# The last layer's modulations in block 2: one of three units in the first attention and two in the second, instead of two and one

## The chip, the cores and the metric

The kernel is one program on one core of a Trainium2 chip. The metric is the time of one execution on the device in microseconds; less is better. Times are medians of several executions, and one further execution was taken with the hardware profiler.

## The reference, cut to what matters

The model is a chain of two blocks of two layers each, on 256 tokens of width 1024, in float32. In block 2 each layer is an attention mixer followed by a hierarchical mixture of experts (MoE), and both are modulated by six vectors that come from the conditioning vector `c_2` alone:

```
cs = jax.nn.silu(c)
for l in range(DEPTH):                       # DEPTH = 2
    mod = (cs @ ada_w[l] + ada_b[l])[:, None, :]
    sh1, sc1, g1, sh2, sc2, g2 = jnp.split(mod, 6, axis=-1)
    h = rms_norm_2(x, norm1_g[l]) * (1.0 + sc1) + sh1
    y = even_mixer_2(...) if l % 2 == 0 else odd_mixer_2(...)
    x = x + g1 * y
    h = rms_norm_2(x, norm2_g[l]) * (1.0 + sc2) + sh2
    x = x + g2 * hier_moe(h, ...)
```

`ada_w[l]` is 1024 x 6144. Nothing in `mod` depends on the tokens, so the product for layer 1 can be computed at any time before layer 1 needs it: `sh1` and `sc1` when layer 1 begins, `g1` when its mixer is added to `x`, and `sh2`, `sc2` and `g2` when its MoE begins.

## The kernel before, in words

Block 2 runs `layerB(0)` (mixer `even2`: four pairs of MoBA heads, four differential heads) and then `layerB(1)` (mixer `odd2`: NSA attention in eight head pairs). In each, the mixer is followed by `out2`, the output projection with the router, and then by the MoE. A head pair consists of score matmuls (`causal_scores`, lines L1561 to L1584; the matmul itself is on L200), a softmax on ScalarE (exponentials, L1581) and VectorE, TensorE transposes of the probabilities (L1592) with VectorE copies (L1593), and value matmuls (L200 with a 64-row `po` tile, or L1643 in the differential heads). In `odd2` the value matmuls read the probabilities from `PT` in the even pairs and from `x` in the odd ones.

The product `cs @ ada_w[l]` is made by generators in three **units**. A unit is one call of `ada_wide`: eight loads of 1 MB (`wraw<-in_bdaU`, from SyncE's queue), and for each load four matmuls of 32 x 512 (`ada<-wraw,csil`, L247), which stand on four column groups of the array. That makes 32 matmuls a unit; the trace holds two records for each, so 64. After every second matmul the generator yields, which is one **step**: 16 steps a unit. Unit 0 (`mods2`) gives `sh1` and `sc1` as columns. Units 1 and 2 (`wide_rows`) give `g1`, `sh2` and then `sc2`, `g2` as rows: VectorE adds the bias (`adb`, L284, for unit 2 also L290) and GpSimd's queue writes the rows to DRAM (`rows_bda`, L293), from where `gates`, `mo_c` and `mo_row` are loaded.

`causal_scores` advances the generator that stands in `self.side` by some steps, `tick(steps, i)`, and each matmul of those steps is put behind the score matmul `i` on TensorE. `even2` calls it 16 times with 2 steps, then with 2 steps in the first two differential heads (4 calls) and with 0 in the last two; `flush()` behind the mixer runs the unit that is under way to its end, and `do()` runs all that is left. `odd2` calls it 16 times with 3 steps. `self.ada2(1)` is started when layer 0 begins and is kept in `self.side` through both layers.

The final order of each engine's instructions isn't the order of the code: the framework's scheduler sorts them along a timeline of its own, and what the code fixes are data dependences, the anchors of `tick` and the buffers of the pools. Two pools matter here. `wr` has ten buffers of 1 MB for all weights, in order of use. `pa` has two PSUM banks (`ada` tiles), of which a unit holds one until its result is read, and the head pairs use the same two for their `po`.

Of the kernel before, what the change touches and what calls it, by code (L numbers as in the profile page):

```python
# [17 lines left out]
P = 128  # L18
# [1483 lines left out]
class B2(L1):  # L1502
# [15 lines left out]
    def ada2(self, l):  # L1518

        yield from self.mods2(l)  # L1520
        r = self.A[f"bdab_r{l}"]
        yield from self.wide_rows(f"bda{l}", 1, self.cs2, (2, 3), r[0], None, None, (0,))
        yield from self.wide_rows(f"bda{l}", 2, self.cs2, (4, 5), r[1], r[2], 1.0, (0,))
# [144 lines left out]
    def odd2(self, hT, ph):  # L1668
# [13 lines left out]
        ksw = [self.T(self.ar, [P, 2, S], f"ksw{n}") for n in range(2)]  # L1682
# [34 lines left out]
        qT = self.T(self.ar, [P, 8, S], "nq")  # L1717
# [34 lines left out]
        for q in range(2):  # L1752
            pr = slice(64 * q, 64 * q + 64)
# [16 lines left out]
        for t in range(2):  # L1770
# [3 lines left out]
            sc = self.S2([P, 16, 32])  # L1774
# [23 lines left out]
        for j in range(8):  # L1798
            po = self.T(self.pa, [P, S], "ada")
            if j % 2:  # L1800
                x = self.T(self.ar, [P, 2048], "x8").rearrange("p (h n k s) -> p h n k s", h=2, n=2, k=2)
                PTs = [[x[:, h2, n] for n in range(2)] for h2 in range(2)]
            else:
                PTs = [[self.T(self.ar, [P, 2, S], "PT", bufs=4) for _ in range(2)] for _ in range(2)]
            hs = [(h2, heads[j][h2], slice(64 * h2, 64 * h2 + 64)) for h2 in range(2)]
            for t in range(2):
                sc = self.causal_scores(t, [[(qT[pr, j, t * P:(t + 1) * P], ksw[n][pr, j // 4, :]) for n in range(2)] for _, _, pr in hs], 3)
                for (e, rs), (h2, h, _) in zip(sc, hs):
                    nc.vector.tensor_tensor(rs, rs, gt[:, t, h * 3 + 1:h * 3 + 3], ALU.mult)
                    for n in range(2):  # L1810
                        nc.vector.tensor_scalar(e[:, n, :], e[:, n, :], rs[:, n:n + 1], None, ALU.mult)
                        self.transp(e[:, n, :], t, PTs[h2][n])
            mm = self.chain()
            for step in range(5):
                for h2, h, pr in hs:
                    g, r = h // 4, h % 4
                    if step == 2:
                        q = slice(32 * r, 32 * r + 16)
                        mm(po[pr, :], vc[q, g, :], PcT[q, g, :], start=False, stop=False, tile_position=(32 * r, 64 * h2), skip_group_check=True)
                    else:  # L1820
                        n, kt = step % 3, step // 3
                        mm(po[pr, kt * P:], vsw[n][:, kt, g * 64:g * 64 + 64], PTs[h2][n][:, kt, kt * P:], start=step == 0, stop=step == 4,
                           tile_position=(0, 64 * h2), skip_group_check=True)
            nc.scalar.activation(mh[:, j, :], po, AF.Copy)
            nc.vector.tensor_tensor(ml[:, j, :], po, mh[:, j, :].bitcast(F32), ALU.subtract)
# [273 lines left out]
    def layerB(self, l):  # L2099
        nc, A = self.nc, self.A  # L2100
        xs = self.xs[:2]
        with self.phase() as ph:
            self.ar = ph.pool(f"arB{l}")
            self.ws = ph.pool(f"wsB{l}", 2)
            Ac, Bc = self.bmods[l]
            if l == 0:
                self.at, self.side = "unit", self.ada2(1)
            hT = self.norm_mod_T(xs, Ac, Bc, [0, 0], rs=self.rn)
            mix = (self.even2 if l == 0 else self.odd2)(hT, ph)
            if l:  # L2110
                self.do(self.side)
            else:
                self.flush()
            G = self.T(self.ar, [P, D], "gates", bufs=1)
            self.row(G, f"bda{l}", 2, 0)
            logits = self.out2(mix, A["b_out"] if l == 0 else A["n_out"], xs, G, *self.router(l))
        with self.phase(ns2=5) as ph:
            self.ar = ph.pool(f"arM{l}")
            hs = [self.T(self.ar, [P, 2, D], n, F32R) for n in ("mo_hh", "mo_hl")]
            xd = [self.T(self.ar, [P, KT, 256], "mo_xd", bufs=2) for _ in range(1)]  # L2120
            hb = [self.T(self.ar, [P, D], f"mo_h{t}") for t in range(2)]
            rows = []
            for b in (4, 3, 5):
                rows.append(self.T(self.ar, [P, D], f"mo_row{b}"))
                self.row(rows[-1], f"bda{l}", b, 0)
            if l:
                fg = self.T(self.ar, [P, D], "mo_fin")
                nc.gpsimd.dma_start(fg, A["fin_g"].partition_broadcast(P))
                self.fin = fg, hb
            self.rn = self.moe(xs, l, logits, rows, hb, *hs)  # L2130
            if l:
                for t in range(2):
                    if t:
                        nc.vector.tensor_scalar(hb[t], hb[t], self.rn[t], None, ALU.mult)
                    else:
                        nc.scalar.activation(hb[t], hb[t], AF.Copy, scale=self.rn[t])  # L2136
                    nc.sync.dma_start(self.out[t * P:(t + 1) * P, :], hb[t])
# [54 lines left out]
```

## Time and profile before

| | |
|---|---|
| median of 3 executions | 2209.05 us (2208.09 to 2222.83) |
| the profiled execution | 2220.42 us |
| its span, first to last instruction | 2218.6 us |
| TensorE matmuls busy | 2024.2 us, 91% of the span |
| VectorE, ScalarE, GpSimd busy | 55%, 38%, 6% |
| mean granted TensorE clock | 0.92 of full speed |

The profiled execution is one among those that spread over 0.7%; durations are read from it and differences are applied to the median. A busy TensorE isn't a TensorE at its peak: the ends of its matmuls are modelled and overlap.

### The profile page before, as it was taken

The page shows a single profiled execution, that of the slowest core. Times are in us where ns is not written, and L with a number is a line of the kernel's source. Part 1 is how long each engine was busy: PE and PEld are TensorE (multiplying, and loading weights), DVE is VectorE, ACT ScalarE, POOL GpSimd, SP SyncE. Part 2 cuts the span into 40 slices and gives each one's busy share as a digit, 9 for nine tenths or more (in the row PEclk, how much of TensorE's full clock was granted, in tenths as well). Part 3 has the DMA queues.
Part 4 walks back from the last instruction along what each step waited for, and adds up shares of the span by engine and source line. Part 5 has one row for each costly group of instructions (what it writes and reads, how often), then busy time and mean ns, then how long its engine had stood idle before and what let it go on. Part 6 is the DMA issues. An engine that isn't in the chain of part 4 may idle for free. (4 is left out here: it accounts for less than half of the span.)

```text
span 2218.6 us, 32046 instructions
## 1 busy us (share of the span) xinstructions
PE 2024.2 (91%) x12738; PEld 1436.3 (65%) x12738; DVE 1219.3 (55%) x2508; ACT 832.4 (38%) x1609; POOL 123.4 (6%) x229
## 2 busy tenths in 40 slices
PE   7999899999989997999987699989989989989896
PEld 4864688888866576765655589978464458546542
DVE  2247565655675645874846555666652244754423
ACT  4334443322353355565434454444341133322211
POOL 1100000001121000000110000000000010000000
PEclk8999999999999998569998899999979999968898
DMA  7546223345532345547984545364748957602494
GB/s 297 140 165 251 95 95 143 143 171 190 209 116 95 109 138 181 152 144 237 297 261 137 205 152 190 143 255 146 267 172 322 386 205 261 222 1 95 196 378 167
DMA packets 124947, 417.44 MB, mean 188 GB/s; under 512 B 19536, under 2 KB 58096, under 8 KB 90096
## 3 DMA queue, kind: packets, MB, share of 16 engines
q1 hardware_dynamic: 54064, 314.86, 38.1%
q10 hardware_dynamic: 55552, 50.95, 7.5%
q0 software_dynamic: 15168, 49.44, 6.6%
q8 instruction: 104, 1.70, 0.3%
q14 instruction: 59, 0.48, 0.1%
HBM read 386.31 MB, written 28.89 MB: 187 GB/s over the span
## 5 line engine op out<-in xcount | busy, mean ns | idle before, releaser
L192 DVE TENSOR_TENSOR wlo<-wraw,whi 128x1024 fp32r<-128x1024 f32 x252 | 308.3, 1226 | 326.6 <-ACT whi L189 326.1
L189 ACT ACTIVATE whi<-wraw 128x1024 fp32r<-128x1024 f32 x252 | 265.7, 1059 | 494.9 <-PE mm L217 236.5
L215 PE MATMUL mm<-hT_h,whi 128*128 128x256 f32 (+1 forms) x832 | 267.7, 333 | 2.5 <-ACT whi L189 2.4
L216 PE MATMUL mm<-hT_l,whi 128*128 128x256 f32 (+1 forms) x832 | 267.8, 329 | 0.0
L217 PE MATMUL mm<-hT_h,wlo 128*128 128x256 f32 (+1 forms) x832 | 242.2, 327 | 1.6 <-DVE wlo L192 1.4
L215 PEld LDWEIGHTS mm<-hT_h,whi 128*128 128x128 f32 x832 | 157.6, 191 | 20.2 <-ACT whi L189 4.1
L216 PEld LDWEIGHTS mm<-hT_l,whi 128*128 128x128 f32 x832 | 158.7, 191 | 14.8
L217 PEld LDWEIGHTS mm<-hT_h,wlo 128*128 128x128 f32 x832 | 149.5, 191 | 18.0 <-DVE wlo L192 3.2
L216 PE MATMUL mm<-wlo,b 128*128 128x512 f32 x384 | 151.7, 395 | 0.6 <-DVE wlo L192 0.6
L217 PE MATMUL mm<-whi,b 128*128 128x512 f32 x384 | 151.3, 394 | 0.0
L2040 PE MATMUL ada<-wraw,mo_xd 128*64 128x512 f32 x512 | 135.5, 599 | 0.0
L215 PE MATMUL mm<-whi,b 128*128 128x512 f32 x384 | 135.4, 394 | 0.0
L247 PE MATMUL ada<-wraw,csil 128*32 128x512 f32 x512 | 103.7, 635 | 12.3 <-DMA wraw<-in_bdaU 10.7
L402 PE MATMUL tr<-s,x 128*128 128x128 f32 x288 | 56.4, 344 | 51.2 <-DVE s L393 25.1
L216 PE MATMUL mm<-wlo,hT_h 128*128 128x512 f32 (+1 forms) x256 | 100.0, 393 | 1.5 <-DVE wlo L192 1.4
L215 PE MATMUL mm<-whi,hT_h 128*128 128x512 f32 (+1 forms) x256 | 95.9, 401 | 1.9 <-ACT s L627 1.4
L217 PE MATMUL mm<-whi,hT_l 128*128 128x512 f32 (+1 forms) x256 | 96.3, 389 | 0.0
L402 PEld LDWEIGHTS tr<-s,x 128*128 128x128 f32 x288 | 49.5, 243 | 62.5 <-issue 37.6
L216 PEld LDWEIGHTS mm<-wlo,b 128*128 128x128 f32 x384 | 72.2, 188 | 18.7 <-DVE wlo L192 1.8
L215 PEld LDWEIGHTS mm<-whi,b 128*128 128x128 f32 x384 | 72.3, 188 | 16.7
L217 PEld LDWEIGHTS mm<-whi,b 128*128 128x128 f32 x384 | 72.2, 188 | 16.5
L2040 PEld LDWEIGHTS ada<-wraw,mo_xd 128*64 128x64 f32 x512 | 38.1, 136 | 67.9 <-issue 67.6
(544 smaller groups left out, 3730.5 us busy)
## 6 DMA issues: line engine op xcount, KB each, us to landing
wraw<-in_w SPq DMA_DIRECT2D x64, 1024.0 KB, 4.8
wraw<-in_moe_gu SPq DMA_DIRECT2D x64, 1024.0 KB, 8.2
wraw<-in_moe_d SPq DMA_DIRECT2D x32, 1024.0 KB, 8.1
PT<-in_adaT POOLq DMA_DIRECT2D x48, 512.0 KB, 4.8
wraw<-in_bdaU SPq DMA_DIRECT2D x48, 512.0 KB, 5.1
wraw<-in_bdaU SPq DMA_DIRECT2D x24, 1024.0 KB, 5.0
wraw<-in_adaU SPq DMA_DIRECT2D x16, 1024.0 KB, 7.1
wraw<-in_b_in SPq DMA_DIRECT2D x12, 1024.0 KB, 8.3
```

What stands on the lines that cost most here:

```text
L189: nc.scalar.activation(h, src, AF.Copy)
L192: self.low = nc.vector.tensor_tensor(l, src, h.bitcast(F32), ALU.subtract)
L215: mm(ps, ah, bh, start=first, stop=False)
L216: mm(ps, ah, bl, start=False, stop=False)
L217: mm(ps, al, bh, start=False, stop=last)
L247: i = nc.tensor.matmul(ps[q:q + 32, :], lhs[:, k, :], raw[:, c % self.wn, :], start=k == 0, stop=k == KT - 1, tile_position=(0, q))
L402: nc.tensor.matmul(pt[:, j, :], xs[e + j][:, k * P:(k + 1) * P], dall[:, e + j, :], start=True, stop=True)
L2040: nc.tensor.matmul(pg[64 * e:64 * e + 64, :], xd[:, k, s0:s0 + 64], gu[e](k), start=k == 0, stop=k == KT - 1, tile_position=(0, 64 * e))
```

## The change

It splits `ada2` so that units 1 and 2 are a generator of their own (`rows2`). Layer 0 starts only unit 0 of layer 1's modulations, 16 steps, and the flush behind `even2` becomes a `do`, which finds nothing left. Layer 1 starts units 1 and 2, 32 steps, and `odd2` asks for 4 steps a call instead of 3. The matmuls, loads and row writes of the three units stay the same in kind and number.

```diff
     def ada2(self, l):
 
         yield from self.mods2(l)
+        yield from self.rows2(l)
+
+    def rows2(self, l):
         r = self.A[f"bdab_r{l}"]
         yield from self.wide_rows(f"bda{l}", 1, self.cs2, (2, 3), r[0], None, None, (0,))
         yield from self.wide_rows(f"bda{l}", 2, self.cs2, (4, 5), r[1], r[2], 1.0, (0,))
...
-                sc = self.causal_scores(t, [[(qT[pr, j, t * P:(t + 1) * P], ksw[n][pr, j // 4, :]) for n in range(2)] for _, _, pr in hs], 3)
+                sc = self.causal_scores(t, [[(qT[pr, j, t * P:(t + 1) * P], ksw[n][pr, j // 4, :]) for n in range(2)] for _, _, pr in hs], 4)
...
-            if l == 0:
-                self.at, self.side = "unit", self.ada2(1)
+            self.at, self.side = "unit", self.rows2(1) if l else self.mods2(1)
             hT = self.norm_mod_T(xs, Ac, Bc, [0, 0], rs=self.rn)
             mix = (self.even2 if l == 0 else self.odd2)(hT, ph)
-            if l:
-                self.do(self.side)
-            else:
-                self.flush()
+            self.do(self.side)
```

On TensorE, at the end of `even2`, the order before has unit 1 (`ada_13635`) in one piece between the scores of the last differential head and the first matmuls of `out2`; `tr` are transposes of probabilities, `ada<-x,PT` value matmuls:

```order
L200 MATMUL mm_13858<-trib_12439,identb_12438 128x128
L247 MATMUL ada_13635<-wraw_13636,csil_16_107 32x512 x4
L247 MATMUL ada_13635<-wraw_13668,csil_16_107 32x512 x4
L247 MATMUL ada_13635<-wraw_13707,csil_16_107 32x512 x4
L247 MATMUL ada_13635<-wraw_13739,csil_16_107 32x512 x3
L1592 MATMUL tr_13730<-ident_67,s_2765_13715 128x128
L1643 MATMUL ada_13695<-x_2583_13147,PT_13614 128x128 x3
L247 MATMUL ada_13635<-wraw_13739,csil_16_107 32x512
L1592 MATMUL tr_13762<-ident_67,s_2777_13747 128x128 x2
L247 MATMUL ada_13635<-wraw_13944,csil_16_107 32x512 x4
L247 MATMUL ada_13635<-wraw_13950,csil_16_107 32x512 x4
L247 MATMUL ada_13635<-wraw_13956,csil_16_107 32x512 x3
```

At the same place the changed kernel has this (its line numbers are 3 higher):

```order
L200 MATMUL mm_13831<-trib_12439,identb_12438 128x128
L1595 MATMUL tr_13709<-ident_67,s_2760_13694 128x128
L1646 MATMUL ada_13680<-x_2583_13147,PT_13614 128x128 x2
L215 MATMUL mm_13946<-whi_13950,hT_h_13292 128x512
L216 MATMUL mm_13946<-wlo_13951,hT_h_13292 128x512
L217 MATMUL mm_13946<-whi_13950,hT_l_13293 128x512
```

Unit 1 is gone from there, and the matmuls of `out2` (`mm_13946`) stand right behind the scores.

On TensorE, in `odd2`, the value matmuls of the second head pair stand before as follows, with no step of a unit among them (the one unit of this attention, `ada_18505`, lies wholly ahead of the first pair's value matmuls):

```order
L200 MATMUL ada_18618<-x_3879_18619,vsw_3683_17510 64x256
L1592 MATMUL tr_18726<-ident_67,s_3904_18702 128x128 x2
L200 MATMUL ada_18618<-x_3879_18619,vsw_3683_17510 64x256
L200 MATMUL ada_18618<-x_3879_18619,vsw_3684_17511 64x256
L1592 MATMUL tr_18785<-ident_67,s_3921_18769 128x128
L200 MATMUL ada_18618<-x_3879_18619,vsw_3684_17511 64x256
```

In the changed kernel the first of the two units (`ada_18449`) lies where that unit lay, and the second one (`ada_18720`) here:

```order
L200 MATMUL ada_18568<-x_3869_18569,vsw_3673_17456 64x256
L247 MATMUL ada_18720<-wraw_18721,csil_16_107 32x512 x4
L247 MATMUL ada_18720<-wraw_18727,csil_16_107 32x512 x4
L247 MATMUL ada_18720<-wraw_18777,csil_16_107 32x512 x4
L247 MATMUL ada_18720<-wraw_18783,csil_16_107 32x512 x4
L1595 MATMUL tr_18682<-ident_67,s_3895_18658 128x128 x2
L247 MATMUL ada_18720<-wraw_18851,csil_16_107 32x512
L200 MATMUL ada_18568<-x_3869_18569,vsw_3673_17456 64x256
L200 MATMUL ada_18568<-x_3869_18569,vsw_3674_17457 64x256
L1595 MATMUL tr_18751<-ident_67,s_3915_18735 128x128
L247 MATMUL ada_18720<-wraw_18851,csil_16_107 32x512 x3
L247 MATMUL ada_18720<-wraw_18857,csil_16_107 32x512 x4
```

All 32 matmuls of the second unit now stand between the first value matmul of the second pair and the next scores; the pairs behind it have none, as before.

## Rows read from the trace of the kernel before

**Rows 1.** The page: busy time by engine, and the granted TensorE clock in 40 slices

```profile
PE 2024.2 (91%) x12738; PEld 1436.3 (65%) x12738; DVE 1219.3 (55%) x2508; ACT 832.4 (38%) x1609; POOL 123.4 (6%) x229
...
PEclk8999999999999998569998899999979999968898
```

**Rows 2.** Windows: busy us by engine, clock, DMA share; the tail of `even2`, then `odd2`

```profile
core 0: us, PE busy (x) PEld busy (x) DVE busy (x) ACT busy (x) POOL busy (x), PEclk, DMA share, GB/s
1596.38:1608.24 11.86, 11.86 (x84) 4.08 (x83) 6.42 (x29) 3.25 (x14) 0.00 (x0) 1.00 0.88 354
1913.04:1933.82 20.78, 20.25 (x124) 7.09 (x123) 15.00 (x65) 6.57 (x30) 0.00 (x0) 0.87 0.84 320
1933.82:1948.80 14.98, 12.35 (x80) 6.75 (x78) 11.64 (x44) 5.79 (x25) 2.08 (x3) 1.00 0.37 121
1959.96:2005.59 45.63, 42.84 (x153) 19.66 (x153) 20.82 (x77) 10.30 (x43) 0.00 (x0) 0.50 0.00 1
...
1936.77:1948.80 12.03, 9.66 (x60) 4.93 (x59) 9.69 (x39) 4.91 (x21) 1.51 (x2) 1.00 0.23 67
...
1961.72:1978.77 17.05, 15.66 (x58) 7.38 (x57) 8.10 (x29) 4.04 (x17) 0.00 (x0) 0.50 0.00 0
```

**Rows 3.** Windows of the steps' matmuls alone (L247): busy us, clock, DMA share

```profile
1596.38:1608.24 11.86, 9.50 (x64) 2.02 (x64) 1.00 0.88 354
1913.04:1933.82 20.78, 12.06 (x64) 2.31 (x64) 0.87 0.84 320
```

**Rows 4.** Timeline, tail of `even2`: start, us, engine, line, tiles, count, [idle before <-releaser]

```profile
1596.38 3.63 PE L247 MATMUL ada<-wraw,csil 128*32 128x512 f32 x30
...
1607.15 0.38 ACT L1644 ACTIVATE ob<-ada 128x256 f32<-128x256 f32 x1 [5.34 <-PE ada L1643]
...
1608.24 0.50 PE L215 MATMUL mm<-whi,hT_h 128*128 128x512 f32 x1
...
1620.71 1.41 PE L1658 MATMUL tr<-ident,ob 128*128 128x128 f32 x4 [3.99 <-DVE ob L1654]
```

**Rows 5.** Timeline of TensorE in `odd2`: the only unit, then the head pairs

```profile
1913.04 5.35 PE L247 MATMUL ada<-wraw,csil 128*32 128x512 f32 x24
1918.32 0.50 PE L200 MATMUL mm<-ksw,nq 64*128 64x128 f32 x4
...
1932.84 1.05 PE L247 MATMUL ada<-wraw,csil 128*32 128x512 f32 x4
...
1947.80 0.70 PE L200 MATMUL mm<-ksw,nq 64*128 64x256 f32 x2 [1.46 <-ACT s L1581]
...
1953.80 0.33 PE L1592 MATMUL tr<-ident,s 128*128 128x128 f32 x1
...
1959.96 1.22 PE L200 MATMUL mm<-ksw,nq 64*128 64x256 f32 x2 [1.16 <-ACT s L1581]
```

**Rows 6.** Timeline of GpSimd's queue in layer 0, and of SyncE's in layer 1

```profile
1609.34 1.12 POOL L293 DMA_DIRECT2D rows_bda<-adb  x2 [140.96 <-DVE adb L284]
...
1619.00 1.60 POOL L371 DMA_DIRECT2D mo_row<-rows_bda  x3
...
1840.28 43.41 SPq L179 DMA_DIRECT2D wraw<-in_bdaU  x8
...
1916.74 8.27 SPq L179 DMA_DIRECT2D wraw<-in_moe_gu  x4
```

**Rows 7.** Timeline, layer 1: router matmul that needs unit 2's rows

```profile
2033.27 0.56 PE L1860 MATMUL ada<-mo_wr,mo_c 128*1 128x20 f32 x16
```

## The prediction

> **What bounds the kernel now.** I read the page first. TensorE is busy 91% of the span at a clock that is granted at nearly full speed, except in a few slices; the one at 6 tenths that begins at 1941 us lies where `odd2` runs [rows 1]. So a unit that leaves or enters the path moves the end by what it takes of TensorE, unless TensorE waits there for something else. Two stages are touched, and I read them by windows and timeline.
>
> In the tail of `even2` the unit is on the path. TensorE is busy in all of 11.86 us between the last differential head's scores and the first matmul of `out2`, at full clock, while VectorE is busy for 6.42 of them [rows 2]. ScalarE waits 5.34 us there for a value matmul that is queued behind the steps [rows 4]. The steps' own matmuls take 9.50 us of that stretch [rows 3].
>
> In `odd2` three things are to be seen. The one unit of this attention fills the stretch up to 1933.82, where TensorE is busy 20.25 of 20.78 us [rows 2], and takes 12.06 us of it at a mean clock of 0.87 [rows 3]. Then the pairs run without steps: 12.03 us for a pair at full clock, with TensorE and VectorE busy for the same 9.7 us each [rows 2] and a longest wait of 1.46 us [rows 5]. And from 1959.96 on, for 45.63 us, the granted clock is 0.50, which is 1.2 GHz, and a pair takes 17.05 us, of which TensorE is busy 15.66 [rows 2]. It fell there in a stretch with waits of 1.16 us [rows 5], 26.1 us after the last step had ended (1932.84 + 1.05).
>
> **The change part by part.** The totals of matmuls, loads and row writes are the same, so the sum is made of what each move takes off and puts on the path.
>
> *Unit 1 leaves the tail of `even2`.* 64 records take 9.50 us [rows 3]. Their cover is nil, since TensorE has no idle time in that stretch [rows 2]: minus 9.5 us. What is late next is the softmax on VectorE. Of the stretch it needs 6.42 us [rows 2], so if `out2` could hide none of it the gain would be 11.86 - 6.42 = 5.4 us; but `out2`'s first matmuls, which don't wait for these heads, now stand right behind the scores, and I stay near TensorE's end: -9.5, with -5.4 as the other end. The wait of 3.99 us behind it, for the normalisation of the heads on VectorE [rows 4], is not shortened; it moves forward as a whole.
>
> *A second unit enters `odd2`.* The first unit keeps its place and its price. The second one costs what 64 records cost there: 12.06 us as the first unit did at 0.87 [rows 3], 9.50 at full clock [rows 3], and 64 x 5.28 / 24 = 14.1 us if all of them run as the first 24 did (1913.04 to 1918.32, 0.22 us each) [rows 5]. Against the price stand TensorE's own waits in a pair, 12.03 - 9.66 = 2.4 us [rows 2], so the low end is 9.5 - 2.4 = 7.1. These waits lie mostly before the unit's new place, at the scores, so I take nothing off, and I take the middle price, because the unit begins about where the clock is unsteady before: +12.1, ends 7.1 and 14.1.
>
> *The clock behind the new unit.* After the last step at 1933.82 the stretch up to 1948.80 ran at 1.00 [rows 2], that is 14.98 us. If the second unit buys the same, the clock holds 15 us from the end of the second pair's value matmuls (1953.80 before) instead of the 6.16 us up to 1959.96 [rows 5]: 8.8 us more at full clock, for work that took 8.8 x 17.05 / 12.03 = 12.5 us. That is -3.7. The ends are 0, if the clock falls as early as now, and 45.63 x (1 - 12.03 / 17.05) = -13.4, if it holds through all of that stretch.
>
> *Queues.* GpSimd's row write waited 140.96 us in layer 0 for the unit, and the loads of `mo_row` stood behind it until 1619.00 [rows 6], well before the MoE. They now come earlier, which is worth 0. In layer 1 `gates`, `mo_c` and `mo_row` stand behind the two row writes; the first that needs them is the router matmul at 2033.27 [rows 7], some 80 us after the second unit's place, so 0 here too, and if that cover were gone the price would be the few us of one load. SyncE's queue has eight more 1 MB loads ahead of `in_n_out` and the experts' weights. Before, the eight loads of the one unit were issued between 1840.28 and 1883.7 and the next ones up to 1916.74 and beyond [rows 6], and from 1959.96 the DMA share is 0.00 [rows 2]: there is room to fetch the weights of `out2` and the experts later. 0, and a late load would show as a wait of TensorE for `wraw`.
>
> *The sum.* -9.5 + 12.1 - 3.7 = -1.1 us. The profiled execution took 2220.42 us, 11.4 above the median of 2209.05; applied to the median this gives **2207.9 us**. That is a twentieth of 1%, and 1% (22 us) is about what a measurement of this kernel can tell from no change.
>
> **The rivals.** *The second unit keeps the clock up for all remaining pairs.* For it: the clock was at 1.00 behind the first unit. Against it: the pairs behind the second unit have no steps, like those that fell. The price of the unit is then the one at full clock: -9.5 + 9.5 - 13.4 = -13.4, 2195.7 us.
>
> The Trainium skill, page "TensorE: Matmul & The Clock Gate", section "Why this matters for your kernels", speaks for this rival: it puts a fall of the clock down to idle gaps between matmul bursts, and names a gap longer than any here. The trace speaks against it, since the clock fell in a stretch whose longest wait was 1.46 us [rows 5], and the measurement decides; hence the smaller chance.
>
> *Slower: the clock is lost earlier and the second unit runs at 1.2 GHz.* The changed order draws all the first unit's steps into the first four score groups, so the last step comes some 7 us earlier than 1933.82 (the four last records of 1.05 us and the waits between). If the clock then holds the same 14.98 us, it falls 7 us earlier, which costs 7 x (17.05 / 12.03 - 1) = 2.9 us; the second unit costs 14.1, and nothing is gained behind it: -9.5 + 14.1 + 2.9 = +7.5, 2216.6 us. It decides as soon as the second unit begins at 0.50 and doesn't bring the clock back. For it: the first 24 records of the first unit ran at half speed [rows 5]. Against it: within that unit the clock came back.
>
> *The gain in `even2` isn't there, because VectorE's softmax sets the end of the tail.* For it: VectorE is busy for 6.42 of 11.86 us there while it waits for TensorE [rows 2]. Against it: the order puts matmuls that need none of it in between. -5.4 + 12.1 - 3.7 = +3.0, 2212 us.
>
> That the change does nothing at all is excluded by the order: the unit has left one attention and stands in the other.
>
> **How the numbers follow.** The forecast, a near balance, gets 0.5; the clock that holds 0.2; the slower case 0.17; VectorE as the bound 0.1; 0.03 is left for what I don't see. All four lie within 1%. The ends of the terms give -9.5 + 7.1 - 13.4 = -15.8 and -5.4 + 14.1 + 2.9 = +11.6, which is 2193 to 2221; the executions before spread from 2208.09 to 2222.83, so I leave the upper end there and say 2194 to 2221. Faster by over 1% would take more than all favourable ends together, slower by over 1% twice the unfavourable ones: 0.03 each, and 0.94 for within 1%.
>
> **What would show each step right or wrong.** In the changed kernel's profile the stretch from the last differential scores to the transposes of `ob`, 24.33 us before (1596.38 to 1620.71) [rows 4], should be about 15 us at a clock near 1.00; 19 would be VectorE as the bound. In `odd2` the second unit should take 9.5 to 14 us between the second pair's value matmuls, and the clock behind it tells the rivals apart: about 15 us at 1.00 and then 0.50 for the forecast, 1.00 up to `out2` for the faster one, 0.50 within the unit and behind it for the slower one. The prediction would be wrong if the scheduler's new order moved the clock in the MoE stages, if TensorE waited for `wraw` in `odd2`, or if the head pairs waited for the PSUM bank that the second unit holds.

## The result

The changed kernel takes 2188.98 us (median of 4 executions, 2181.55 to 2203.59) against 2214.99 us (4 executions, 2208.09 to 2222.83) for the kernel before, measured on the same chip: a ratio of 0.9877, 95% interval 0.983 to 0.9923. It is faster by 1.2%, outside the predicted range and on a side that had been given 0.03. The forecast stood on 2209.05 us, the median of three executions; with a fourth the median is 2214.99, and the forecast's -1.1 us would make 2213.9 of that. The profiled execution of the changed kernel took 2203.59 us, the slowest of its four; further profiles of both kernels stand below. Ratios leave out executions more than 1.5% above the fastest of their kernel, which concerns four of the twelve of `before4` alone.

The page of the changed kernel, its busy times and the granted clock in 40 slices, the counterpart of [rows 1]. The slice at 6 tenths, the 36th before, now reads 9, and TensorE is busy 10 us less:

```profile
PE 2014.0 (91%) x12738; PEld 1434.8 (65%) x12738; DVE 1216.7 (55%) x2508; ACT 832.7 (38%) x1609; POOL 123.8 (6%) x229
...
PEclk9999999999989999569988999999989999998898
```

Windows of the changed kernel, the counterparts of [rows 2]: the tail of `even2`, which now opens with the first matmul of `out2`, the first unit in `odd2`, the stretch from the second to the third pair's value matmuls with the second unit in it, and the two pairs behind it:

```profile
core 0: us, PE busy (x) PEld busy (x) DVE busy (x) ACT busy (x) POOL busy (x), PEclk, DMA share, GB/s
1600.31:1608.24 7.93, 7.68 (x43) 6.37 (x42) 6.13 (x22) 4.60 (x13) 0.00 (x0) 1.00 0.01 2
1908.05:1926.80 18.75, 18.27 (x135) 7.74 (x134) 16.01 (x67) 7.98 (x39) 1.13 (x2) 0.89 0.82 326
...
1938.30:1955.01 16.71, 16.38 (x121) 6.24 (x120) 9.46 (x37) 3.85 (x18) 1.10 (x2) 1.00 0.99 400
1955.01:1966.76 11.75, 9.68 (x60) 4.94 (x59) 9.47 (x39) 4.92 (x21) 0.93 (x1) 1.00 0.58 238
1966.76:1978.13 11.37, 10.07 (x56) 4.77 (x55) 7.24 (x28) 3.96 (x17) 0.00 (x0) 0.81 0.01 1
```

The first of these two, the third pair, took 11.75 us at 1.00, where it took 17.05 us at 0.50 before [rows 2]; the clock falls within the fourth.

Windows of the changed kernel for the steps' matmuls alone (L247), up to the first pair's value matmuls of the compressed part and in the second unit's place; 64 records each, as in [rows 3]:

```profile
1903.15:1931.65 28.50, 9.57 (x64) 2.06 (x64) 0.88 0.72 286
1938.30:1955.01 16.71, 8.53 (x64) 1.90 (x64) 1.00 0.99 400
```

Timeline of TensorE in the changed kernel, tail of `even2`, the counterpart of [rows 4]: `out2`'s first matmul, value matmuls of the last differential head, and the transposes of `ob`, which still wait 3.93 us:

```profile
1600.36 0.48 PE L215 MATMUL mm<-whi,hT_h 128*128 128x512 f32 x1
...
1609.38 0.46 PE L1646 MATMUL ada<-x,PT 128*128 128x128 f32 x2 [0.52 <-DVE PT L1596]
...
1615.22 1.47 PE L1661 MATMUL tr<-ident,ob 128*128 128x128 f32 x4 [3.93 <-DVE ob L1657]
```

Timeline of TensorE in the changed kernel's `odd2`, where [rows 5] had no step: the second unit stands among the second pair's value matmuls, in four pieces, and there is no wait among them:

```profile
1938.30 0.65 PE L200 MATMUL ada<-x,vsw 128*64 128x256 f32 x2
1938.88 3.64 PE L247 MATMUL ada<-wraw,csil 128*32 128x512 f32 x32
...
1942.82 1.04 PE L247 MATMUL ada<-wraw,csil 128*32 128x512 f32 x2
...
1944.64 2.78 PE L247 MATMUL ada<-wraw,csil 128*32 128x512 f32 x24
...
1949.46 1.06 PE L247 MATMUL ada<-wraw,csil 128*32 128x512 f32 x6
```

One profile of a kernel turned out to be one draw among several, so the kernel before was profiled five times and the changed one four times. The table gives the means over these profiles, stage by stage; a stage runs from the first TensorE instruction of its kind to that of the next.

| stage | before, 5 profiles | changed, 4 profiles | difference |
|---|---|---|---|
| the first 878 us, not touched | 877.9 | 878.0 | 0.1 |
| from there to 1285 us, not touched | 407.3 (405.5 to 409.8) | 404.5 (399.2 to 409.1) | -2.8 |
| up to `even2`'s scores, not touched | 263.9 | 263.9 | 0.0 |
| `even2`, first scores to the transposes of `ob` | 71.22 (71.21 to 71.24) | 61.77 (all four) | **-9.45** |
| `out2`, the MoE of layer 0, begin of `odd2` | 288.5 | 287.7 | -0.8 |
| `odd2`, scores against the compressed keys to `out2`'s transposes | 131.5 | 122.3 | **-9.2** |
| `out2` and MoE of layer 1 | 173.1 | 173.0 | -0.1 |
| span | 2213.4 | 2191.2 | -22.2 |

Two stages carry the gain, 9.45 us in `even2` and 9.2 us in `odd2`, although `odd2` now holds a unit more. The 2.8 us of the second row come from code that is the same in both; its spread between executions of one kernel is larger than that. All executions taken together, 61 of the kernel before and 12 of the changed one, have means of 2215.9 and 2191.4 us.

### The profile page after: what moved, and what is told of

Its sections match the earlier page's. It is cut to its first block, busy times and chain, and to the rows that moved or that the text cites. A ratio compares the mean times of both kernels' runs of the same rounds, so it can differ in the third digit from the quotient of the medians.

```text
span 2201.8 us, 32051 instructions
## 1 busy us (share of the span) xinstructions
PE 2014.0 (91%) x12738; PEld 1434.8 (65%) x12738; DVE 1216.7 (55%) x2508; ACT 832.7 (38%) x1609; POOL 123.8 (6%) x229
## 5 line engine op out<-in xcount | busy, mean ns | idle before, releaser
L247 PE MATMUL ada<-wraw,csil 128*32 128x512 f32 x512 | 99.1, 632 | 13.3 <-DMA wraw<-in_bdaU 11.7
```

The costliest lines, as they stand in the source:

```text
L247: i = nc.tensor.matmul(ps[q:q + 32, :], lhs[:, k, :], raw[:, c % self.wn, :], start=k == 0, stop=k == KT - 1, tile_position=(0, q))
```

## The experiments

Each timed kernel was compared with executions of the kernel before on the same chip; ratios are to those. The values of a pair, where a stretch begins or ends at them below, are its value matmuls of the compressed part (`ada<-g,vcT`), which stand in the middle of its value matmuls. "Behind the third pair" means: from there in the third head pair to the transposes of `out2`. In both kernels this stretch holds 344 records of matmuls and no step of a unit. Their order differs a little from the fifth pair on, but with the same 27.3 us at the lower clock the stretch took 74.1 us before and 73.3 in the changed kernel, so its length is in the main a reading of the clock. The two levels of the granted clock are 1.00 (2.4 GHz) and 0.50 (1.2 GHz).

**again** (the changed kernel, not edited, timed once more).

> The changed kernel once more, for an interval and a second profile. Clock theory (the steps in odd2 keep TensorE at 2.4 GHz for the head pairs behind them, so the second unit pays for itself): about 2189 us, ratio 0.985 to 0.992, and in the profile the stretch in odd2 from the compressed scores (kcT) to the first transposes of out2 again near 125 us against 136 before. Path theory (a unit costs its 9.5 to 12 us of TensorE wherever it stands, and the rest of the gain was the spread between executions): ratio near 1.00, and that stretch near 136 to 140 us.

Measured: 2192.56 us (2185.98 to 2199.61, 6 executions), ratio 0.9899 (0.9867 to 0.9932). The gain is there again. Its `odd2` took 128.6 us, 3.5 more than the first profile's 125.1.

**before4** (steps of the kernel before: only the number changes).

```diff
-for _, _, pr in hs], 3)
+for _, _, pr in hs], 4)
```

> The kernel before with 4 steps a call in odd2 instead of 3: the one unit there is drawn ahead into the first four groups of scores, nothing else moves. Packing theory (the earlier and denser first unit gives some 5 us, since the first pair's value matmuls came 3.1 us and the second pair's 5.5 us earlier in the changed kernel): 5 us shorter, ratio 0.998. Clock theory in its simple form: the last step comes 7 us earlier, so the clock falls earlier and the pairs behind it are the slower ones: 0 to 3 us longer.

Measured: 2218.18 us (2189.57 to 2225.14, 12 executions), ratio 0.9975 (0.9939 to 1.0011). Drawing the steps of the one unit together isn't the whole gain; the 5 us of the packing theory are not excluded. Its profile is of one of its faster executions, 2202.51 us, and has 123.8 us for `odd2` and 67.8 behind the third pair, both within what the changed kernel shows, although no second unit stands there. So the clock behind the third pair can also hold longer without one.

**after2** (the changed kernel with `4` put to `2` in that line, which asks for the steps over all 16 calls; in the trace 40 of the second unit's 64 records stand among the fourth pair's value matmuls and the rest ahead of the fifth and the sixth pair's).

> The changed kernel with 2 steps a call in odd2: the 32 steps are spread over all 16 calls, so that nearly every head pair has some of them. Clock theory: the granted clock stays near 1.00 through all pairs, the two pairs that still ran at 0.50 to 0.77 gain up to 5 us each: 3 to 8 us shorter than the changed kernel. Path theory: the same number of matmuls, so the same time within 2 us. If it is longer, single steps cost more than a lump, or the PSUM bank that the units hold through all pairs is what counts.

Measured: 2189.02 us (2186.08 to 2199.09), ratio 0.9881 (0.9852 to 0.991), `odd2` 120.2 us. The same time as the changed kernel's, where 3 to 8 us less had been expected of the clock: at these two places of the second unit the kernel takes the same time.

**dup** (the kernel before, with unit 1 made a second time in `odd2` and 4 steps: `odd2` holds two units as in the changed kernel, and `even2` keeps its own).

```diff
+            else:
+                self.side = chain(self.wide_rows("bda1", 1, self.cs2, (2, 3), A["bdab_r1"][0], None, None, (0,)), self.side)
```

> The kernel before, which in odd2 makes unit 1 a second time (same values, same rows written twice) with 4 steps a call; even2 keeps its unit 1. So it has 32 matmuls and eight loads more than either kernel, and odd2 as in the changed kernel. Clock theory: odd2 still gets shorter, by about 11 us, ratio near 0.995. Path theory: 9.5 to 12 us longer, ratio 1.004 to 1.006. Against the changed kernel it prices the removal from even2 alone: 9.5 us by the trace.

Measured: 2211.64 us (2206.98 to 2227.8), ratio 0.9979 (0.9953 to 1.0004). A whole unit more in `odd2`, with nothing taken away anywhere, costs nothing that can be measured. By the step of the prediction that priced it, this kernel should have been some 12 us slower, or 8 with the gain in clock put down for it. But it is also some 20 us slower than the changed kernel, where taking unit 1 out of `even2` explains 9.45. In its two profiles, of executions that are slower than its median, the rest is in `odd2`, 135.8 and 138.6 us against 117.8 to 128.6: the clock falls there already in the first pair, as windows of its first profile show, where the changed kernel has 1.00 (the second row begins 26.6 us behind the compressed scores in both):

```profile
1918.33:1943.33 25.00, 24.19 (x161) 12.37 (x160) 18.64 (x71) 7.96 (x36) 1.19 (x2) 0.86 0.71 277
1944.90:1965.40 20.50, 20.05 (x77) 9.11 (x80) 12.94 (x42) 6.52 (x23) 0.63 (x1) 0.50 0.35 132
```

The same windows of the changed kernel:

```profile
1903.15:1928.15 25.00, 23.94 (x175) 13.06 (x174) 20.31 (x80) 9.11 (x43) 1.13 (x2) 0.86 0.68 269
1929.70:1950.20 20.50, 19.95 (x143) 7.79 (x141) 12.49 (x41) 7.73 (x28) 0.59 (x1) 1.00 0.80 319
```

So `dup` isn't the changed kernel's `odd2` behind the old `even2`, as I had meant it to be: its scores and transposes ahead of the first pair's values are sorted a little differently. That this order is why the clock falls there is not shown.

**late1** (the changed kernel, but the second unit stands behind the pairs, and 3 steps a call for the first).

```diff
-            self.at, self.side = "unit", self.rows2(1) if l else self.mods2(1)
+            self.at, self.side = "unit", self.rows2(1, (0,)) if l else self.mods2(1)
...
             self.do(self.side)
+            if l:
+                self.do(self.rows2(1, (1,)))
```

> The changed kernel with the second unit taken out of odd2's pairs and made behind them, beside the last pair's values; the first unit is issued three steps at a time as in the kernel before, so the pairs run in the order of the kernel before. Theory of the clock (the second unit costs little in the pairs because it fills TensorE's waits and keeps the clock up): the pairs fall back to the kernel before's mix of clocks and the unit costs its full 9 to 10 us at the end, so 8 to 18 us over the changed kernel's 2192, that is 2200 to 2210. Theory of the path (the unit costs its own time wherever it stands, and the gain is even2's alone): no difference to the changed kernel beyond 3 us, 2189 to 2196.

Measured: 2193.25 us (2189.48 to 2197.86, 7 executions), ratio 0.989 (0.9858 to 0.9922): no difference to the changed kernel. My theory of the clock said 2200 to 2210 and is refuted in this form: the second unit need not stand among the pairs. Its profile shows why. The scheduler sorted its pairs in another way, although their code is that of the kernel before: the next pair's scores stand between the value matmuls of the pair under way. From 1942 us on, its timeline of TensorE has one wait in a pair, as in these two:

```profile
1945.38 0.64 PE L1597 MATMUL tr<-ident,s 128*128 128x128 f32 x3 [0.28 <-DVE PT L1598]
...
1954.64 0.64 PE L1597 MATMUL tr<-ident,s 128*128 128x128 f32 x3 [0.28 <-DVE x L1598]
```

The longest wait in such a pair is 0.28 us, a pair takes 9.2 to 9.3 us, and windows of it up to the third pair's values and behind show the clock at 1.00 throughout the second:

```profile
1899.62:1952.76 53.14, 50.52 (x311) 24.73 (x312) 41.28 (x155) 20.33 (x84) 3.21 (x5) 0.94 0.50 194
1952.76:2019.42 66.66, 65.72 (x398) 37.21 (x397) 36.64 (x114) 19.00 (x60) 1.17 (x3) 1.00 0.35 137
```

The unit isn't free at the end: from the seventh pair's values to `out2`'s transposes it is 26.4 us here and 18.9 in the kernels before and after, 7.5 us more. The stage of `out2` and the MoE behind it takes 175.7 us instead of 173.1 too, because the unit's rows come late: its timeline has a wait there, which neither kernel has, for the router weights that VectorE makes from `mo_c`.

```profile
2027.89 2.32 PE L1911 MATMUL ada<-mo_wa,s 128*128 128x20 f32 x10 [2.44 <-DVE mo_wa L1862]
```

The quicker pairs pay for both.

**late1_4** (late1 with 4 steps instead of 3). The units stand as in late1; the scheduler sorts the pairs in blocks again, as in the kernels before and after.

> The kernel with the second unit behind odd2's pairs, now with four steps a call for the first unit. Work and places of the units are those of late1, but the scheduler's order of the pairs is another: as in the kernels before and after, the value matmuls of a pair stand in one block and the next pair's scores in another, where late1 has the scores between the value matmuls. Theory of the order (scores between the value matmuls keep TensorE busy and its clock up; blocks let it fall): odd2's pairs spend 20 to 50 us at 1.2 GHz and the time is 5 to 14 us over late1's 2193, 2198 to 2207. If the order doesn't matter and the gain comes from the second unit having left even2 alone: 2190 to 2197, like late1.

Measured: 2201.62 us (2186.5 to 2215.08, 10 executions), ratio 0.9947 (0.9906 to 0.9987). The median lies where the theory of the order put it, and the executions spread over 28.6 us where late1's spread over 8.4. The two intervals overlap, and the execution that was profiled was one of the shortest (2190.87 us), with only 3.4 us at 1.2 GHz among the pairs. So the order of the pairs is likely to matter, but this pair of kernels doesn't show it beyond doubt. Its timeline shows what blocks do to TensorE. Two pairs in a row have a wait of 0.54 us and one of 1.16; these are the second pair's:

```profile
1958.60 0.49 PE L200 MATMUL mm<-ksw,nq 64*128 64x128 f32 x2 [0.54 <-ACT s L1586]
1961.54 0.70 PE L200 MATMUL mm<-ksw,nq 64*128 64x256 f32 x2 [1.16 <-ACT s L1586]
```

**fill_before** (the kernel before with a useless matmul into each bank of scores of `odd2`, which the scores overwrite).

```diff
         kw = dict(skip_group_check=True)
+        for b in banks[:fill]:
+            mm(b.rearrange("p a b -> p (a b)"), self.ident, self.rp.rearrange("p a b -> p (a b)")[:, 0:n * W], start=True, stop=True, **kw)
```

> The kernel before, with one useless matmul of identity by rope table (f32, 128 by 256 or 128 by 512) into each bank of scores in odd2 ahead of the scores, which overwrite it: 32 matmuls and no unit moved. Theory of the clock: odd2's stretch at 1.2 GHz, 51 us in the profiled execution of the kernel before, falls under 20 us and the time falls by 3 to 12 us against the kernel before (2205 to 2214), although work is added. Theory of the path: the work is added to the path, 32 matmuls of 0.35 to 0.7 us, 5 to 20 us slower (2222 to 2237), at an unchanged clock.

Measured: 2201.99 us (2197.24 to 2208.97, 10 executions), ratio 0.9945 (0.9919 to 0.9971). Thirty-two matmuls of no use make the kernel 0.55% faster, a little more than the theory of the clock had put down. Windows of it, as above: more TensorE work than the kernel before in both rows (352 and 350 records against 301 and 344), and the clock at 1.00 in both:

```profile
1900.90:1960.16 59.26, 58.39 (x352) 28.52 (x351) 40.66 (x153) 18.73 (x84) 2.08 (x3) 1.00 0.37 143
1960.16:2022.94 62.78, 60.97 (x350) 36.48 (x350) 36.21 (x114) 19.00 (x60) 2.11 (x4) 1.00 0.17 57
```

That refutes the theory of the path, by which every matmul added is time added. It doesn't say which of two things held the clock, since in this kernel too the scheduler put the scores between the values.

**fill_after** (the same useless matmuls in the changed kernel, in pairs 4 to 7 alone, `fill = 2 if j >= 4 else 0`).

> The changed kernel with the same useless matmuls in pairs 4 to 7 alone, where its own profile shows the clock fall at 1977 to 1990 us. Theory of the clock: that fall goes or shrinks, and the time is between 8 us faster and level (2184 to 2192). Theory of the path: 16 matmuls of 0.35 to 0.7 us more, 4 to 10 us slower (2196 to 2202).

Measured: 2192.16 us (2187.68 to 2203.13, 4 executions), ratio 0.9877 (0.9821 to 0.9934): level with the changed kernel. In its profile the clock stays at 1.00 behind the third pair, in 65.8 us, where the changed kernel took 62.5 at that clock. So what the filler may save in clock it costs in work, as far as one profile shows it.

**after3** (the changed kernel with 3 steps).

> The changed kernel with three steps at a time instead of four, which spreads the second unit over pairs 1 to 4. Theory of the clock: work spread over more pairs holds the clock about as well, 2186 to 2196, and the stretch at 1.2 GHz in odd2 stays under 30 us. If it is the crowding of the first unit under the first scores that saves the time, this kernel loses 5 us or more, 2197 or over.

Measured: 2194.26 us (2189.36 to 2200.39, 4 executions), ratio 0.9897 (0.9839 to 0.9955); `odd2` 121.0 us, at 1.00 from 9.1 us on. In its trace the second unit stands among the second pair's value matmuls and ahead of the third's, near its place in the changed kernel. With after2 and late1 it makes three kernels of different order or place of the units that all take about the changed kernel's time; none beats it by more than these measurements can tell.

**before_b, before_c, before_d, before_e, after_b, after_c, dup_b** (kernels not edited, one profile each).

> The kernel before, unchanged, for a second profile of its odd2. Theory of the order: again 30 to 60 us of odd2 at 1.2 GHz, and 130 to 140 us from the first scores against the compressed keys to out2's transposes (136.4 in the first profile). If the first profile was an unlucky execution: under 126 us.

> The kernel before, third profile. If odd2's clock carries the rest of the gain: odd2 at 127 to 138 us with 27 us or more at 1.2 GHz behind its first 10 us. If another stage carries it: odd2 under 124 us, and a stage outside odd2 and even2 that is longer than in the changed kernel.

> The kernel before, fourth profile, to the same question as the third: odd2 at 127 to 138 us if its clock carries the rest of the gain, under 124 us if another stage does.

> The kernel before, fifth profile, to the same question as the third: odd2 at 127 to 138 us if its clock carries the rest of the gain, under 124 us if another stage does.

> The changed kernel for a third profile: odd2 at 120 to 129 us, with the clock at full speed in the first three pairs and 7 to 34 us of odd2 at 1.2 GHz in the later ones.

> The changed kernel, fourth profile: odd2 at 117 to 129 us; a mean of the four near 123 would leave 8 to 12 us of the gain to odd2.

> The kernel before with unit 1 made once more in odd2, for a second profile: does the fall of the clock during the first pair (26.6 to 47.0 us behind the first scores against the compressed keys) come back? Theory of the order: yes, odd2 at 132 to 138 us. Chance: under 128 us, as in the changed kernel.

Measured: the executions took 2216.01, 2217.81, 2206.0 and 2216.32 us (before), 2189.69 and 2187.4 us (changed) and 2215.86 us (dup), and `odd2` 127.2, 136.4, 128.8 and 128.8, then 117.8 and 117.8, and 138.6 us. Three of these missed what was expected: before_b's 127.2 lies between its two views, after_b's 117.8 came without the fall of the clock that was put down for the later pairs, and dup_b's 138.6 lies just above its range. Windows of `odd2` up to the third pair's values and behind them, in the first profile of the kernel before:

```profile
1908.67:1965.89 57.22, 52.36 (x301) 24.80 (x301) 39.93 (x154) 18.94 (x84) 2.08 (x3) 0.85 0.40 148
1965.89:2045.02 79.13, 75.26 (x344) 43.05 (x343) 37.88 (x115) 19.52 (x60) 2.12 (x4) 0.74 0.13 46
```

In before_d, which before_e repeats to within 0.01 us:

```profile
1902.24:1956.94 54.70, 49.84 (x302) 24.28 (x302) 39.09 (x151) 18.95 (x84) 2.08 (x3) 0.91 0.41 154
1956.94:2031.09 74.15, 69.97 (x344) 40.77 (x343) 38.43 (x118) 19.42 (x60) 2.12 (x4) 0.82 0.14 48
```

In again, the worst of the changed kernel's four:

```profile
1887.95:1943.22 55.27, 52.80 (x365) 25.45 (x365) 41.47 (x154) 20.44 (x84) 5.06 (x8) 0.94 0.79 314
1943.22:2016.54 73.32, 70.10 (x344) 40.83 (x343) 38.34 (x118) 19.43 (x60) 2.29 (x5) 0.81 0.19 67
```

In after_b, which after_c repeats to within 0.03 us:

```profile
1897.30:1952.59 55.29, 52.82 (x366) 25.32 (x366) 41.59 (x154) 20.44 (x84) 4.85 (x8) 0.94 0.78 314
1952.59:2015.11 62.52, 58.53 (x344) 36.09 (x344) 38.08 (x118) 19.26 (x60) 2.45 (x5) 1.00 0.22 80
```

The second rows are to be compared: the 344 records take 62.5 us at 1.00, 73 to 74 us at 0.81 to 0.82 and 79.1 us at 0.74. The five profiles of the kernel before gave 79.13, 74.12, 79.13, 74.15 and 74.15 us, the four of the changed one 69.83, 73.32, 62.52 and 62.49: means of 76.1 and 67.0, a difference of 9.1 us, with no unit's work in it. The time at 1.2 GHz in this stretch was 41.2, 27.3, 41.2, 27.3 and 27.3 us before, and 17.1, 27.3, 0 and 0 after. The first rows hold the whole cost of the second unit: some 65 records more, yet 55.3 us in each profile after against 57.22, 53.05, 57.24, 54.70 and 54.70 before, means of 55.3 and 55.4.

## Why the prediction was wrong

**The first term was right.** Unit 1 leaving `even2` was put at -9.5 us; the stage is 9.45 us shorter in every profile. From the last differential scores to the transposes of `ob` it was 24.33 us [rows 4] and is now 14.9 (with the first scores of the stage aligned), as the forecast's mark said, and VectorE didn't become the bound: the wait for `ob` merely moved forward, 3.99 us to 3.93.

**The step that failed is "a second unit enters `odd2`", +12.1 us with 7.1 as the low end.** Up to the third pair's value matmuls the two kernels take the same time. Three things make up the difference, read in before_d and the first profile after:

- The second unit costs +3.7 us net: from the first to the third pair's values 26.8 us instead of 23.1 (against the two profiles before in which this stretch took 25.7 us, +1.1). Its 64 records are busy for 8.53 us at full clock, not 12.06. Windows of that stretch, in before_d and in the changed kernel:

```profile
1933.84:1956.94 23.10, 19.40 (x113) 9.68 (x113) 15.76 (x59) 7.92 (x34) 0.94 (x1) 0.93 0.02 1
1931.65:1958.44 26.79, 25.55 (x178) 10.88 (x177) 18.21 (x63) 9.68 (x36) 1.83 (x3) 1.00 0.85 344
```

  TensorE stands idle in it for 3.70 us before and 1.24 after, 2.5 us less of waiting. I had measured those waits (2.4 us in a pair) but taken nothing off for them, since the order puts the unit behind the scores. Not only waits beside the unit got shorter; whether the unit did that, or the closer first unit ahead of it, isn't shown: in before4, without a second unit, the same stretch has 0.54 us of idle time, at a mean clock of 0.72. The fall of the clock that all five profiles before show some 40 us behind the compressed scores (0.93 in the first row) isn't there after, where the unit stands at that place; it is inside the net figure too.
- The first unit didn't keep its price. With 4 steps a call its records are busy 9.57 us instead of 12.02, and the first pair's values begin 28.50 us behind the compressed scores instead of 31.60: -3.1 us. The steps' matmuls alone (L247), in before_d:

```profile
1902.24:1933.84 31.60, 12.02 (x64) 2.31 (x64) 0.89 0.70 267
```

  In before4 the records are busy 9.18 us, yet the first pair's values begin 32.0 us behind the compressed scores; there the clock fell at 24.8 us and stayed low beyond them.
- 12.1 was the price of the unit at the place of the first one, where the clock is at a half for part of the time; the place of the second one ran at 1.00.

**The term for the clock behind the new unit was right in direction and mis-sized:** -3.7 us put down, -9.1 us measured (means of five and four profiles), with ends between 74.1 - 73.3 = 0.8 and 79.1 - 62.5 = 16.6. That the second unit is what holds the clock isn't shown: late1 and before4 have no second unit ahead of that stretch, and it takes 66.7 us there, with 7.5 for the unit at its end, and 67.8. I had the clock hold for 15 us more, and then fall. In two profiles out of four it held for all remaining pairs, in two it fell at 63.6 to 63.8 us behind the compressed scores, and in the kernel before it had fallen at 38 to 40 us and again at 51 to 64, in each of five profiles.

**The sum as measured** is -9.45 in `even2`, -0.1 up to the third pair in `odd2`, -9.1 behind it and -0.8 between the two stages (of which one profile before, with 290.0 us, makes about half): -19.4 us, where the forecast had -1.1. The spans differ by 22.2 us and the means of all executions by 24.5; of what is left, 2.8 us stand in untouched code.

The granted clock is on record for every execution of both kernels but four, and by an estimate it accounts for the rest. By it 57 executions of the kernel before spent 342 us at 1.2 GHz in the mean, and the 12 of the changed one 299. Among executions of the same kernel, 1 us more at 1.2 GHz goes with 0.34 us more time (a straight line through both kernels' executions, each about its own mean). So 42.5 x 0.34 = 14.4 us (95% interval 10 to 19) of the 24.5 go with the clock, and the other 10.2 us (7 to 13) are about what `even2` gave, 9.45. On that reckoning the second unit in `odd2` cost next to nothing beyond the clock, and the clock, which the forecast had at -3.7, is the largest term of all.

**The rivals.** The faster one had the right direction and came nearest, 2195.7 us, but for a part of the reason: the clock holds to the end in half of the profiles only, and the unit costs less than the 9.5 us it allowed. The Trainium skill, page "TensorE: Matmul & The Clock Gate", section "Why this matters for your kernels", stood beside it with the rule that the clock falls after idle gaps between matmul bursts, and names a gap longer than any in `odd2`. The runs come near the rival's time but don't bear out that rule: in again the clock fell in `odd2`, 63.6 us behind the compressed scores, with no wait of more than 1.16 us ahead of it in that stage. The slower rival, the clock lost within the second unit, didn't occur in any profile of the changed kernel; something like it did in dup, whose clock fell in the first pair.

**What stays open** is what decides whether the clock falls. Work that fills TensorE's waits (fill_before) and an order without waits of 1.16 us (late1, after3) go with a clock that holds, and the four kernels with scores between the values (after2, after3, late1, fill_before) had 6.9 us or less of `odd2` at 1.2 GHz, all of it in the first 10 us, in one profile each. But so had two of the changed kernel's four profiles, with waits of 1.16 us, fill_before changed both at once, and late1_4 against late1 isn't decisive. So why the clock falls less often in the changed kernel is open; that it does, and what that is worth, is measured.

## What to carry to other kernels

A movable unit of work costs its own duration where TensorE has no waits, and less where it has some: it gave back all of it in `even2` (9.45 us), cost a part of it among the pairs of `odd2` (1.1 to 3.7 of 8.5 us), and 7.5 us behind the pairs, with 2.5 more for its rows coming late. Where the granted clock isn't 1.00 in a stretch, price the move of work by what it does to the clock of everything behind it, and give that term its full range: here 0.8 to 16.6 us, more than the move itself. Profile the kernel before several times ahead of such a prediction; one profile is one draw, and my 45.63 us at the lower clock were of the longer of two stretches that the same kernel shows, some 48 us in two profiles and 27 in three.

## What I had not expected of the hardware

The same instructions at the same times can be followed by either clock. In again and after_b, the same kernel, the stretch from the third pair's values to the wait of 1.16 us agrees to 0.02 us on TensorE and VectorE; from 1.0 us behind that wait's end the one runs 27.3 us at 0.50 and the other goes on at 1.00. Windows of again:

```profile
1943.22:1950.54 7.32, 5.62 (x42) 3.23 (x41) 5.66 (x21) 2.94 (x13) 0.17 (x1) 1.00 0.46 186
1951.55:1978.85 27.30, 26.77 (x97) 12.65 (x97) 13.05 (x48) 7.06 (x30) 0.00 (x0) 0.50 0.00 1
```

The same stretches in after_b, 9.35 us later in its span:

```profile
1952.57:1959.89 7.32, 5.63 (x42) 3.23 (x41) 5.64 (x21) 2.94 (x13) 0.35 (x1) 1.00 0.46 186
1960.90:1988.20 27.30, 26.01 (x153) 15.13 (x153) 19.21 (x67) 10.96 (x41) 0.00 (x0) 1.00 0.07 19
```

And the outcomes aren't spread evenly but repeat: `odd2` took 136.36 and 136.37 us in two profiles of the kernel before and 128.85 and 128.84 us in two others, and 117.81 and 117.78 us in two of the changed kernel; the other three profiles, 127.2, 125.1 and 128.6 us, stand alone. A median of few executions then depends on how often each outcome was drawn.
